# First layers of the compressions with 32 activation columns stationary on four column groups

## The chip, the core and the metric

The kernel runs on one core of one Trainium2 chip. The metric is the device time of one execution in microseconds; the times shown are the median of several executions, and a profile is one execution taken apart by the hardware profiler. The engines are named as the profile names them: PE is TensorE (PEld its weight loads), ACT ScalarE, DVE VectorE, POOL GpSimd, SP the engine that issues most transfers.

## The reference, cut to what matters

Two decoder layers on 512 positions of 1024 values. Each layer has an FFN, a mixer of three kinds of attention, a second FFN and an embedding gate. In the mixer, the NSA heads attend to compressed keys and values too. Each of 31 blocks (32 positions, a new one every 16) becomes one key and one value:

```
def compress(kv, pe, w1, w2):
    blk = kv[:, idx] + pe[:, None, :]
    blk = jnp.transpose(blk, (0, 1, 3, 2, 4)).reshape(B, n_cmp, NSA_KV_HEADS, CMP_BLOCK * HEAD_DIM)
    return jax.nn.gelu(blk @ w1) @ w2
kc = rope(compress(k_cmp, pos_k, phi_k1, phi_k2), block_end)
vc = compress(v_cmp, pos_v, phi_v1, phi_v2)
```

`blk @ w1` is the first layer: 31 rows (padded to 32) by 2048, times 2048 by 256. There are four of them in an execution: keys and values, in two layers. They are computed in full four-byte precision.

## The kernel before

Most products of the kernel split a four-byte operand into a high and a low part and add three products of a faster four-byte type. The first layers of the compressions don't: their operands are plain four-byte values, for which a matmul leaves two records in the trace, each with its own weight load.

The mixer (from L559) is written as a list of short steps, `SEQ`; the steps of one layer are written out in that order, and a scheduler then sets the order on each engine by priority and by when it holds inputs and buffers to be free. Each engine runs its own list strictly in that order. The steps that matter here:

- `cmp` (L800): projects the values to be compressed and lays them out as `xs`, sixteen slices of 128 by 32 for keys and for values.
- `hk0` to `hk3` and `hv0` to `hv3`: `phi(i, j)` (L819), a quarter of the first layer each. A step takes one weight unit of 128 by 1024 (`wraw`, loaded over SP into a buffer of its own) with four blocks of 256 columns. Before the change, each half block of 128 columns is stationary and 32 columns of `xs` move, eight matmuls per step, 32 per compression. All add up in one PSUM tile with tag "g", of which there are two; the projections and the compressed scores use the same two. Behind the last quarter VectorE takes the sums out as `gx` (L831) and a tanh GELU runs in nine small steps over VectorE and ScalarE (L834 to L846), which gives `g`.
- `ck` and `cv`: the second layers (`phik` with `gx`, `phiv` with `g`); `ck` gives `kp`, `cv` gives `vc`.
- `cs` and `ct`: the scores of the compressed keys (`nq`,`kp`), their softmax (`scr`, `sc`) and its transposition (`pct`). `pct`,`vc` is added to the output of an NSA head in the step `Pn0b`.
- `Q..`, `T..`, `P..`: scores and softmax, transposes and output product of a head. Names with n, d, f are NSA, differential and forgetting heads; `nk`,`nq` are the scores of NSA heads, `PT`,`VN` their output products, `ident`,`P` the transposes.
- `Gf..`, `Gd..`: the projection of a head, 24 matmuls of 512 columns (`xh`,`whi` and the like). `Gd0` is followed by a rotation: ScalarE copies to `raw_r` (L732), two transfers write `rot`, VectorE multiplies and adds (L735 to L737), ScalarE and VectorE split into `dhi` and `dlo`.

The steps between `hk2` and `Gf2` stand in `SEQ` as: hk2 hk3 Gf3 Qn1a hv0 hv1 ck Qn1b hv2 Tn0b Tn0a Pf1 Pn0a cs Gd0 hv3 ct Qn2a Qn2b Tn1b Qn3a cv Pn0b Tn1a Pn1a Qn3b Gf2.

Small working tiles come from a pool `tmp` of four buffers: `raw_r`, `rot`, `dhi`, `dlo`, `scr`, `sc` and others share them.

Of the kernel before, what the change touches and what calls it, by code (L numbers as in the profile page):

```python
# [20 lines left out]
F32 = mybir.dt.float32  # L21
F32R = mybir.dt.float32r
AF = mybir.ActivationFunctionType
# [29 lines left out]
def _mix(w, n):  # L53

    return w.reshape(-1, n, 2, 64 // n).transpose(0, 2, 3, 1).reshape(-1, 128)
# [61 lines left out]
def _consts():  # L117
    c = {}
    c["ident"] = np.eye(128, dtype=np.float32)
    q = np.arange(128)  # L120
    m = np.zeros((128, 512), np.float32)
    m[:, 384:] = np.where(q[None, :] <= q[:, None], 0.0, NEG)
    c["mask"] = m
    ut = np.ones((128, 512), np.float32)
    ut[:, :128] = (q[:, None] <= q[None, :])
    c["ut"] = ut

    def table(d, pos):
        inv = (np.float32(10000.0) ** (-np.arange(0, d, 2, dtype=np.float32) / np.float32(d))).astype(np.float32)
        ang = pos.astype(np.float32)[:, None] * inv[None, :]  # L130
        co, si = np.cos(ang).astype(np.float32), np.sin(ang).astype(np.float32)
        n = 128 // d
        return [np.ascontiguousarray(_mix(np.tile(np.concatenate(x, 1), (1, n)), n).T)
                for x in ((co, co), (-si, si))]

    t = np.arange(S)
    c["rope"] = np.stack([*table(64, t), *table(32, t)])
    be = np.arange(32) * 16 + 31
    c["ropec"] = np.stack(table(64, be), 1)
    ok = (np.arange(32)[None, :] < NCMP) & (be[None, :] <= t[:, None])  # L140
    c["maskc"] = np.where(ok, 0.0, NEG).astype(np.float32).reshape(4, 128, 32).transpose(1, 0, 2)
    c["rowc"] = (t >= 31).astype(np.float32).reshape(4, 128).T
    b = np.zeros((128, 128), np.float32)
    b[:64, :64] = b[64:, 64:] = 1.0 / 64
    c["bd"] = b
    return {k: np.ascontiguousarray(v, np.float32) for k, v in c.items()}


def layout(a):

    a = {k: np.asarray(v) for k, v in a.items()}
    o = dict(_consts())
    o["x"] = a["x"][0]
    o["xt"] = a["x"][0].T.reshape(KC, 128, S).transpose(1, 0, 2)
    o["pt"] = a["p"][:, 0].transpose(0, 2, 1).reshape(L, 2, 128, S).transpose(0, 2, 1, 3)
    o["ws"] = np.stack(_stream(a, 0) + _stream(a, 1))
    o["ln_g"], o["ln_b"], o["bg"] = a["ln_g"], a["ln_b"], a["ple_b_gate"]
    k2 = a["nsa_phi_k2"].reshape(L, 2, 128, 2, 32)
    o["phik2"] = np.stack([np.repeat(x.reshape(L, 2, 128, 64), 2, 3) for x in (k2, k2[..., ::-1, :])], 3).transpose(0, 2, 1, 3, 4)
    o["phiv2"] = a["nsa_phi_v2"].reshape(L, 2, 128, 64).transpose(0, 2, 1, 3)  # L160
    o["pe"] = np.stack([a["nsa_pos_k"], a["nsa_pos_v"]], 1).reshape(L, 2, 16, 128).transpose(0, 3, 1, 2)
    o["bf"] = a["fox_b_f"]
    o["lam"] = a["diff_lambda"].reshape(L, 128)
    o["sg"] = np.concatenate([a["diff_subln_g"]] * 2, 1)
    return {k: np.ascontiguousarray(v) for k, v in o.items()}
# [3 lines left out]
class _Body:  # L169
# [85 lines left out]
    def mm(self, out, l, r, start, stop, loose=False):  # L255

        self.nc.tensor.matmul(out, l, r, start=start, stop=stop, skip_group_check=loose)  # L257
# [361 lines left out]
    def mixer(self, l):  # L619
        nc, A = self.nc, self.A  # L620
# [18 lines left out]
        M = {}  # L639
# [21 lines left out]
        for t in range(NT):  # L661
            p = self.ps("gs"[t % 2])
# [155 lines left out]
        def phi(i, j):  # L818

            if j == 0:  # L820
                M["ps", i] = self.ps("g")
            p = M["ps", i][:, 0:64]
            w = self.unit().rearrange("p (b m n) -> p b m n", b=4, m=2)
            for b in range(4):
                k = 4 * j + b
                for m in range(2):
                    self.mm(p[:, 32 * m:32 * m + 32], w[:, b, m], M["X"][:, i, k], k + m == 0, k == 15, True)
            if j < 3:
                return
            x, y = lw([128, 2, 32], f"gx{i}"), lw([128, 2, 32], f"gy{i}")  # L830
            nc.vector.tensor_copy(x, p.rearrange("p (a b) -> p a b", a=2))  # L831

            c = 2.0 * math.sqrt(2.0 / math.pi)
            nc.vector.tensor_mul(y, x, x)  # L834
            nc.vector.tensor_scalar(y, y, -0.044715 * c, -c, op0=ALU.mult, op1=ALU.add)
            nc.vector.tensor_mul(y, y, x)
            nc.vector.tensor_scalar(y, y, 80.0, None, op0=ALU.min)
            nc.scalar.activation(y, y, AF.Exp)
            nc.vector.tensor_scalar(y, y, 1.0, None, op0=ALU.add)
            nc.vector.reciprocal(y, y)  # L840
            if i == 0:
                nc.vector.tensor_mul(x, x, y)
                M["phi", 0] = x
            else:
                g = M["phi", 1] = lw([128, 2, 4, 32], "g1")
                nc.vector.tensor_mul(g, *(a[:, :, None, :].to_broadcast([128, 2, 4, 32]) for a in (x, y)))  # L846
# [246 lines left out]
        for n in SEQ:  # L1093
            if n[0] == "W":
                out_piece(int(n[1]), int(n[2]))
            elif n[0] == "h":
                phi("kv".index(n[1]), int(n[2]))
            elif n in steps:
                steps[n]()
                if len(M) and all(k in M for k in (("q", 0), ("q", 1), "k")) and "n0" not in M:  # L1100
                    ready()
            else:
                {"G": G, "Q": QS, "T": TP, "P": PV}[n[0]](n[1:])
# [12 lines left out]
        g, b = self.bcast(A["ln_g"][l, 1]), self.bcast(A["ln_b"][l, 1])  # L1116
# [55 lines left out]
    def start(self):  # L1172
        nc, A = self.nc, self.A

        self.ident = self.cp.tile([128, 128], F32, name="ident")
        self.mhalf = self.cp.tile([128, 1], F32, name="mhalf")
        self.one = self.cp.tile([128, 1], F32, name="one")
        self.eps = self.cp.tile([128, 1], F32, name="eps")
        for n in ("mask", "bd", "maskc", "rowc", "ropec"):
            setattr(self, n, self.cp.tile(list(A[n].shape), F32, name=n))  # L1180
        self.xh = self.cp.tile([128, KC, S], F32R, name="xh")
        self.xl = self.cp.tile([128, KC, S], F32R, name="xl")
        nc.vector.memset(self.mhalf, -0.5)
        self.x = [self.h4(F32, name="x") for t in range(NT)]

        z = self.h4(shape=(128, 512), name="zero")
        nc.vector.memset(z.bitcast(F32), 0.0)
        p = self.ps("t")
        for _ in range(self.opt["warm"]):
            self.mm(p, z[:, 0:128], z, True, True)  # L1190

        raw = [self.h4(F32, name="raw") for _ in range(2)]
        for u in range(2):
            self.hl[u] = [self.big(self.tags[u], name="w") for _ in range(2)]
        for k in range(KC):
            r = self.big("h", F32, (128, 512), "xraw")
            x = nc.sync.dma_start(r, A["xt"][:, k])
            if k % 2 == 0:
                c = slice(128 * k, 128 * k + 256)
                for u in range(2):  # L1200
                    self.last_raw = nc.sync.dma_start(raw[u][:, c], A["ws"][u, :, c])
            self.hilo(self.xh[:, k], self.xl[:, k], r)
            if k % 2 == 0:
                for u in range(2):
                    self.hilo(self.hl[u][0][:, c], self.hl[u][1][:, c], raw[u][:, c])
        self.dma_u = self.split_u = 2
        for u in range(2, 4):
            self._load(u)
            self.after(self.last_raw, x)
            self.dma_u += 1  # L1210
        self.ahead(3)
        nc.vector.memset(self.one, 1.0)
        nc.vector.memset(self.eps, EPS)

    def load_x(self):
        nc, A = self.nc, self.A
        for t, n in ((self.ident, A["ident"]), *((self.x[t], A["x"][128 * t:128 * t + 128]) for t in range(NT)),
                     *((getattr(self, n), A[n]) for n in ("mask", "bd", "maskc", "rowc", "ropec"))):
            self.after(nc.sync.dma_start(t, n), self.last_raw)


# [72 lines left out]
```

## Time and profile before

| | us |
|---|---|
| median of 3 executions | 2094.37 (2089.83 to 2094.72) |
| profiled execution, time | 2092.3 |
| profiled execution, span | 2090.5 |
| PE busy | 2068.9 |
| PEld busy | 1840.6 |
| DVE busy | 1443.9 |
| ACT busy | 1107.8 |

The span runs from the first to the last instruction; the time of that execution holds 1.8 us more. The mixer of layer 0 lies at about 380 to 655 us, that of layer 1 at about 1420 to 1695 us. A timeline row gives the start, the duration (of a merged row, from its first start to its last end, with the pipeline's latency), engine, line, operation, output and inputs, shapes and count. On PE, "out<-a,b" has the moving operand first and the stationary second; "128*8" is the size of the stationary block. Because matmuls overlap in the pipeline, the distance of two starts is what a matmul costs, not its duration.

### The profile page before, as it was taken

Reading aid. Unit: us, or ns where it says so; the run is one execution under the profiler, and the core shown is the slowest. Engines: PE = TensorE matmul, PEld = TensorE weight load, DVE = VectorE, ACT = ScalarE, POOL = GpSimd, SP = SyncE. Lnnn points to the kernel's source line nnn. Section 1 sums busy time; section 2 is a strip of 40 time slices with the busy share of each in tenths; the row PEclk is TensorE's granted clock in tenths of the full one; section 3 lists DMA queues with packets and bytes.
Section 4 is the critical chain, followed back from the end, with each engine's and each line's share of the span. In section 5 each row is a group of like instructions: output and inputs, shape, how many; then the busy total and the mean of one; then the engine's idle time right before and its main releaser. Section 6 shows DMA issues by size and latency. Waiting matters only on the chain.

```text
span 2090.5 us, 32936 instructions
## 1 busy us (share of the span) xinstructions
PE 2068.9 (99%) x12727; PEld 1840.6 (88%) x12727; DVE 1443.9 (69%) x2674; ACT 1107.8 (53%) x1947; POOL 128.6 (6%) x165
## 2 busy tenths in 40 slices
PE   9999999999999999999999999999999999999999
PEld 7999888797778999988899998887977789998887
DVE  7797526359888888626768885364688879886275
ACT  5665424457874666513546654244678646664132
POOL 0000001000100000000000000010101000000000
PEclk9999999989999999999999999999999999999999
DMA  5765234544562655324226542355445526553241
GB/s 178 205 173 141 94 111 157 172 134 128 138 199 64 172 158 162 118 94 151 102 71 173 161 132 92 115 168 158 145 121 147 187 65 186 153 142 105 98 151 61
DMA packets 89821, 286.32 MB, mean 137 GB/s; under 512 B 12865, under 2 KB 15041, under 8 KB 89665
## 3 DMA queue, kind: packets, MB, share of 16 engines
q1 hardware_dynamic: 74864, 230.74, 32.2%
q0 software_dynamic: 14800, 53.48, 13.4%
q8 instruction: 100, 1.64, 0.3%
q14 instruction: 57, 0.46, 0.1%
HBM read 209.46 MB, written 6.29 MB: 103 GB/s over the span
## 4 chain that ended last, share of the span: by engine, by line
PE 89%; ACT 4%; DVE 3%; DMA 2%; issue 1%; SPq 0%; DVEq 0%; ACTq 0%; POOLq 0%
PE ps L257 86%; PE ps L951 2%; PE ps L274 1%; ACT whi L221 1%; ACT P L929 1%; DMA rot<-raw_r 1%; DMA raw<-in_ws_dram 1%; DVE wlo L227 1%; ACT PT L249 0%; DMA glo<-raw 0%; PE ps L998 0%; DMA xraw<-in_xt_dram 0%; DVE P L927 0%; DVE PT L250 0%; ACT ob L990 0%
## 5 line engine op out<-in xcount | busy, mean ns | idle before, releaser
L257 PE MATMUL ps<-whi,hl 128*128 128x512 f32 x1376 | 427.9, 390 | 0.0
L221 ACT ACTIVATE whi<-raw 128x1024 fp32r<-128x1024 f32 x198 | 209.3, 1059 | 389.6 <-PE ps L257 313.5
L227 DVE TENSOR_TENSOR wlo<-raw,whi 128x1024 fp32r<-128x1024 f32 x174 | 212.1, 1222 | 294.1 <-ACT whi L221 285.6
L257 PE MATMUL ps<-T,sum 128*128 128x256 f32 x2592 | 335.9, 283 | 0.0
L257 PEld LDWEIGHTS ps<-T,sum 128*128 128x128 f32 x2592 | 321.6, 192 | 1.1 <-ACT sum L388 0.7
L257 PEld LDWEIGHTS ps<-whi,hl 128*128 128x128 f32 x1376 | 257.7, 188 | 54.1 <-DVE hl L250 1.2
L257 PE MATMUL ps<-wlo,hl 128*128 128x512 f32 x704 | 274.1, 389 | 0.0
L391 DVE TENSOR_TENSOR sum<-whole,sum 128x512 fp32r<-128x512 f32 x288 | 194.3, 687 | 28.8 <-ACT sum L388 28.3
L388 ACT ACTIVATE sum<-whole 128x512 fp32r<-128x512 f32 x288 | 174.9, 627 | 49.0 <-DVE whole L426 28.4
L257 PE MATMUL ps<-xh,whi 128*128 128x512 f32 (+1 forms) x536 | 197.1, 370 | 0.8 <-ACT xh L276 0.8
L257 PE MATMUL ps<-xh,wlo 128*128 128x512 f32 (+1 forms) x536 | 195.9, 366 | 0.0
L257 PE MATMUL ps<-xl,whi 128*128 128x512 f32 (+1 forms) x536 | 195.7, 366 | 0.0
L257 PE MATMUL ps<-xh,glo 128*128 128x256 f32 x576 | 163.1, 283 | 0.2 <-DMA glo<-raw 0.2
L257 PE MATMUL ps<-xl,ghi 128*128 128x256 f32 x576 | 163.0, 283 | 0.0
L257 PE MATMUL ps<-xh,ghi 128*128 128x256 f32 x576 | 163.0, 283 | 0.0
L257 PEld LDWEIGHTS ps<-wlo,hl 128*128 128x128 f32 x704 | 132.2, 188 | 27.5
L929 ACT ACTIVATE P<-P,sst 128x128 f32<-128x128 f32 x192 | 106.5, 559 | 40.5 <-DVE sst L927 40.2
L398 ACT ACTIVATE ghi<-raw 128x1024 fp32r<-128x1024 f32 x72 | 76.2, 1058 | 76.7 <-PE ps L257 69.0
L257 PE MATMUL ps<-T,up 128*128 128x256 f32 x864 | 115.4, 283 | 0.0
L257 PE MATMUL ps<-xh,sum 128*128 128x256 f32 x576 | 115.4, 283 | 0.0
L257 PEld LDWEIGHTS ps<-xh,whi 128*128 128x128 f32 x536 | 101.2, 190 | 15.4 <-ACT xh L276 1.5
L927 DVE CUSTOM_DVE_ANT_0 P<-ps,mask 128x128 f32<-128x128 f32 x192 | 88.3, 485 | 38.2 <-PE ps L257 26.5
(245 smaller groups left out, 4033.4 us busy)
## 6 DMA issues: line engine op xcount, KB each, us to landing
raw<-in_ws_dram SPq DMA_DIRECT2D x270, 512.0 KB
P<-in_ws_dram SPq DMA_DIRECT2D x72, 512.0 KB
glo<-raw POOLq DMA_DIRECT2D x71, 512.0 KB, 4.7
wlo<-raw POOLq DMA_DIRECT2D x24, 512.0 KB, 5.1
wraw<-in_ws_dram SPq DMA_DIRECT2D x16, 512.0 KB
dx<-x SPq DMA_DIRECT2D x8, 512.0 KB
x<-dx SPq DMA_DIRECT2D x8, 512.0 KB
rot<-raw_r SPq DMA_DIRECT2D x28, 128.0 KB
```

Of the source, the lines that this page charges most:

```text
L221: self.nc.scalar.activation(hi, r, AF.Copy)
L227: self.nc.vector.tensor_sub(lo, r, hi.bitcast(F32))
L257: self.nc.tensor.matmul(out, l, r, start=start, stop=stop, skip_group_check=loose)
L274: nc.tensor.transpose(p[:, j], self.x[t][:, 128 * k:128 * k + 128], self.ident)
L388: S.activation(Sm[j, i][0], W[j, i], AF.Copy)
L391: V.tensor_sub(Sm[j, i][1], W.pop((j, i)), Sm[j, i][0].bitcast(F32))
L398: S.activation(h, g, AF.Copy)
L927: nc.vector.tensor_tensor_reduce(v, p[:, 0:n], self.mask[:, 512 - n:512], -scale, 3e38, ALU.add, ALU.min, nm[:, t:t + 1])
L929: nc.scalar.activation(v, v, AF.Exp, bias=nm[:, t:t + 1], scale=-1.0, accum_out=sm[:, t:t + 1])
L951: nc.tensor.transpose(p[:, 128 * i:128 * i + 128], P[:, off[t] + 128 * kb:off[t] + 128 * kb + 128], self.ident)
```

## The change

`phi` swaps the operands of the first layer. The 32 columns of `xs` are stationary and a whole block of 256 weight columns moves: four matmuls per step instead of eight. The four blocks of a step write four different groups of 32 PSUM partitions, hence four column groups of the array. Each group adds up its own four of the sixteen slices over the four steps. After the last step ScalarE copies the 128 by 256 sums to a tile `qs` from the pool `tmp`, and two matmuls with `qs` stationary and four stacked identities `four` (128 by 32) moving add the four parts, into another part of the same PSUM tile. The rest is as before. `four` is one more constant, loaded with the others in the first FFN.

```
--- before.py
+++ after.py
@@ -143,6 +143,7 @@
     b = np.zeros((128, 128), np.float32)
     b[:64, :64] = b[64:, 64:] = 1.0 / 64
     c["bd"] = b
+    c["four"] = np.tile(np.eye(32, dtype=np.float32), (4, 1))
     return {k: np.ascontiguousarray(v, np.float32) for k, v in c.items()}
 
 
@@ -819,14 +820,19 @@
 
             if j == 0:
                 M["ps", i] = self.ps("g")
-            p = M["ps", i][:, 0:64]
-            w = self.unit().rearrange("p (b m n) -> p b m n", b=4, m=2)
+            q = M["ps", i][:, 0:256]
+            w = self.unit().rearrange("p (b n) -> p b n", b=4)
+
             for b in range(4):
-                k = 4 * j + b
-                for m in range(2):
-                    self.mm(p[:, 32 * m:32 * m + 32], w[:, b, m], M["X"][:, i, k], k + m == 0, k == 15, True)
+                self.mm(q[32 * b:32 * b + 32], M["X"][:, i, 4 * j + b], w[:, b], j == 0, j == 3, True)
             if j < 3:
                 return
+
+            qs = self.tmp(shape=(128, 256), name="qs")
+            nc.scalar.activation(qs, q, AF.Copy)
+            p = M["ps", i][:, 256:320]
+            for m in range(2):
+                self.mm(p[:, 32 * m:32 * m + 32], qs[:, 128 * m:128 * m + 128], self.four, m == 0, m == 1, True)
             x, y = lw([128, 2, 32], f"gx{i}"), lw([128, 2, 32], f"gy{i}")
             nc.vector.tensor_copy(x, p.rearrange("p (a b) -> p a b", a=2))
 
@@ -1180,6 +1186,7 @@
             setattr(self, n, self.cp.tile(list(A[n].shape), F32, name=n))
         self.xh = self.cp.tile([128, KC, S], F32R, name="xh")
         self.xl = self.cp.tile([128, KC, S], F32R, name="xl")
+        self.four = self.cp.tile([128, 128], F32, name="four")[:, 0:32]
         nc.vector.memset(self.mhalf, -0.5)
         self.x = [self.h4(F32, name="x") for t in range(NT)]
 
@@ -1215,7 +1222,7 @@
     def load_x(self):
         nc, A = self.nc, self.A
         for t, n in ((self.ident, A["ident"]), *((self.x[t], A["x"][128 * t:128 * t + 128]) for t in range(NT)),
-                     *((getattr(self, n), A[n]) for n in ("mask", "bd", "maskc", "rowc", "ropec"))):
+                     *((getattr(self, n), A[n]) for n in ("mask", "bd", "maskc", "rowc", "ropec", "four"))):
             self.after(nc.sync.dma_start(t, n), self.last_raw)
```

The scheduler's order changes from the first compression to the end of each mixer. On PE, layer 0, from `hk1` to the end of `hk3` (`xs`,`wraw` is the old product, `wraw`,`xs` the new one), the kernel before has:

```order
L257 MATMUL ps<-xs,wraw 128x32 x8
L257 MATMUL ps<-nk,nq 128x128
L257 MATMUL ps<-nk,nq 128x256
L257 MATMUL ps<-xs,wraw 128x32 x13
L257 MATMUL ps<-nkl,nq 128x128
L257 MATMUL ps<-nkl,nq 128x256
L257 MATMUL ps<-xs,wraw 128x32 x3
```

In the changed kernel the same stretch of PE's list reads:

```order
L258 MATMUL ps<-wraw,xs 32x256 x4
L258 MATMUL ps<-nk,nq 128x128
L258 MATMUL ps<-nk,nq 128x256
L258 MATMUL ps<-wraw,xs 32x256 x5
L258 MATMUL ps<-nkl,nq 128x128
L258 MATMUL ps<-nkl,nq 128x256
L258 MATMUL ps<-wraw,xs 32x256 x3
```

The counts halve and the shape changes; the score products stand between them at nearly the same places.

On ACT, layer 0, about the rotation of `Gd0` (`raw_r`, `dhi`) and the GELU of the value compression (`gy`, then `vc` from the second layer), the kernel before has:

```order
L249 ACTIVATE oT<-pair 128x512
L895 ACTIVATE sc<-sc 128x512
L732 ACTIVATE raw_r<-ps 128x512
L838 ACTIVATE gy_4845<-gy_4845 128x64
L221 ACTIVATE whi<-raw 128x1024
L224 ACTIVATE wlo<-raw 128x1024
L249 ACTIVATE vc<-ps 128x64
L249 ACTIVATE PT<-ps 128x512 x2
L249 ACTIVATE PT<-ps 128x256
L249 ACTIVATE dhi<-raw_r 128x512
```

In the changed kernel, from the exponentials ahead of `dhi`:

```order
L935 ACTIVATE P,sst<-P,sst 128x384
L250 ACTIVATE PT<-ps 128x512
L935 ACTIVATE P,sst<-P,sst 128x512
L250 ACTIVATE dhi<-raw_r 128x512
L250 ACTIVATE PT<-ps 128x256
L832 ACTIVATE qs<-ps 128x256
L844 ACTIVATE gy_4823<-gy_4823 128x64
L935 ACTIVATE P,sst<-P,sst 128x128
L935 ACTIVATE P,sst<-P,sst 128x256
L250 ACTIVATE pct<-ps 128x512
L935 ACTIVATE P,sst<-P,sst 128x384
L250 ACTIVATE vc<-ps 128x64
```

Before, `gy` and `vc` of the value compression stand ahead of `dhi`; now the copy `qs`, `gy` and `vc` stand behind it.

On PE, layer 0, about the second layer of the value compression (`phiv`). In the kernel before, the end of an output product stands ahead of it and Gf2's projection behind it:

```order
L257 MATMUL ps<-PT,VN 128x128
L257 MATMUL ps<-PT,VN 64x128
L257 MATMUL ps<-phiv,g_4854 128x64 x2
L257 MATMUL ps<-xh,whi 128x512
L257 MATMUL ps<-xl,whi 128x512
L257 MATMUL ps<-xh,wlo 128x512
L907 MATMUL ps<-ident,sc 128x128 x4
L951 MATMUL ps<-ident,P 128x128 x8
```

In the changed kernel `phiv` stands among these:

```order
L258 MATMUL ps<-nkl,nq 128x256
L957 MATMUL ps<-ident,P 128x128 x2
L258 MATMUL ps<-four,qs 128x32 x2
L957 MATMUL ps<-ident,P 128x128 x4
L258 MATMUL ps<-nk,nq 128x384
L258 MATMUL ps<-nkl,nq 128x384
L258 MATMUL ps<-nk,nq 128x512
L258 MATMUL ps<-nkl,nq 128x512
L957 MATMUL ps<-ident,P 128x128 x4
L258 MATMUL ps<-nk,nq 128x128
L258 MATMUL ps<-nkl,nq 128x128
L258 MATMUL ps<-phiv,g_4832 128x64 x2
L258 MATMUL ps<-xh,whi 128x512
```

Before, `Gd0`'s projection ends 13 rows ahead of `phiv` (at row 1643 of the list, `phiv` is row 1656), and transposes and Gf2's projection follow it. Now `Gd0`'s projection ends 33 rows ahead (1647 and 1680): transposes, scores, output products and the identities stand between, and Gf2's projection begins behind `phiv`.

## Rows read from the trace of the kernel before

**Rows 1.** The page, busy time by engine and the chain that ended last.

```profile
PE 2068.9 (99%) x12727; PEld 1840.6 (88%) x12727; DVE 1443.9 (69%) x2674; ACT 1107.8 (53%) x1947; POOL 128.6 (6%) x165
...
PE 89%; ACT 4%; DVE 3%; DMA 2%; issue 1%; SPq 0%; DVEq 0%; ACTq 0%; POOLq 0%
```

**Rows 2.** Groups by form on PE: count, busy us, mean ns, idle before.

```profile
L257 PE MATMUL ps<-xs,wraw 128*128 128x32 f32 x256 | 34.0, 292 | 0.0
```

**Rows 3.** Timeline of PE, 420 to 480 us.

```profile
424.54 1.87 PE L257 MATMUL ps<-xs,wraw 128*128 128x32 f32 x16
426.24 0.31 PE L257 MATMUL ps<-fb,fa 128*128 128x128 f32 x1
```

**Rows 4.** PE by stretch: length, busy us (count), mean granted clock, DMA share, GB/s.

```profile
436.00:448.00 12.00, 12.00 (x67) 0.72 0.59 208
456.00:464.00 8.00, 8.00 (x40) 0.57 0.44 91
478.90:494.40 15.50, 13.94 (x81) 1.00 0.73 188
494.40:616.20 121.80, 117.90 (x640) 1.00 0.49 145
1480.00:1486.00 6.00, 6.00 (x29) 0.72 0.73 251
1494.00:1502.00 8.00, 8.00 (x41) 0.57 0.47 97
1618.00:1620.00 2.00, 0.77 (x2) 1.00 0.77 272
1620.00:1624.00 4.00, 3.98 (x14) 0.57 1.00 212
```

**Rows 5.** Timeline of PE at the decay sum.

```profile
392.50 2.32 PE L257 MATMUL ps<-ut,fz 128*8 128x512 f32 x8
394.75 0.50 PE L257 MATMUL ps<-xh,whi 128*128 128x512 f32 x1
```

**Rows 6.** Timeline of the weight loads (PEld) at the decay sum.

```profile
392.94 0.09 PEld L257 LDWEIGHTS ps<-ut,fz 128*8 128x8 f32 x1 [0.34 <-issue]
393.37 0.09 PEld L257 LDWEIGHTS ps<-ut,fz 128*8 128x8 f32 x1 [0.34 <-issue]
```

**Rows 7.** Timeline of PE, 478 to 496 us.

```profile
478.44 0.39 PE L257 MATMUL ps<-xl,whi 128*128 128x512 f32 x1
478.67 0.39 PE L257 MATMUL ps<-xh,wlo 128*128 128x512 f32 x1
...
479.36 1.32 PE L257 MATMUL ps<-PT,VN 128*128 128x512 f32 x8
481.17 0.66 PE L257 MATMUL ps<-phiv,g 128*128 128x64 f32 x4 [0.49 <-DVE g L846]
...
487.56 0.34 PE L257 MATMUL ps<-nk,nq 128*128 128x384 f32 x1
...
488.37 0.39 PE L257 MATMUL ps<-xl,whi 128*128 128x512 f32 x1
...
494.37 0.50 PE L257 MATMUL ps<-pct,vc 32*128 32x512 f32 x1
```

**Rows 8.** Timeline of ACT, 478 to 490 us.

```profile
481.53 1.06 ACT L221 ACTIVATE whi<-raw 128x1024 fp32r<-128x1024 f32 x1 [1.69 <-DMA raw<-in_ws_dram]
...
487.06 0.38 ACT L249 ACTIVATE PT<-ps 128x256 fp32r<-128x256 f32 x1 [2.44 <-PE ps L951]
487.34 0.62 ACT L249 ACTIVATE dhi<-raw_r 128x512 fp32r<-128x512 f32 x1
```

**Rows 9.** Timeline of DVE, 467 to 482 us: the value compression's GELU.

```profile
467.72 0.23 DVE L831 COPY gx<-ps 128x64 f32<-128x64 f32 x1 [0.87 <-PE ps L257]
...
475.65 0.22 DVE L834 TENSOR_TENSOR gy<-gx 128x64 f32<-128x64 f32 x1
...
480.69 0.42 DVE L846 TENSOR_TENSOR g<-gx,gy 128x256 f32<-128x256 f32 x1
```

More of the change, by code (lines that the diff above doesn't have):

```diff
@@ L145, in _consts @@
     c["bd"] = b
+    c["four"] = np.tile(np.eye(32, dtype=np.float32), (4, 1))
     return {k: np.ascontiguousarray(v, np.float32) for k, v in c.items()}
@@ L821, in phi @@
                 M["ps", i] = self.ps("g")
-            p = M["ps", i][:, 0:64]
-            w = self.unit().rearrange("p (b m n) -> p b m n", b=4, m=2)
+            q = M["ps", i][:, 0:256]
+            w = self.unit().rearrange("p (b n) -> p b n", b=4)
             for b in range(4):
-                k = 4 * j + b
-                for m in range(2):
-                    self.mm(p[:, 32 * m:32 * m + 32], w[:, b, m], M["X"][:, i, k], k + m == 0, k == 15, True)
+                self.mm(q[32 * b:32 * b + 32], M["X"][:, i, 4 * j + b], w[:, b], j == 0, j == 3, True)
             if j < 3:
                 return
+            qs = self.tmp(shape=(128, 256), name="qs")
+            nc.scalar.activation(qs, q, AF.Copy)
+            p = M["ps", i][:, 256:320]
+            for m in range(2):
+                self.mm(p[:, 32 * m:32 * m + 32], qs[:, 128 * m:128 * m + 128], self.four, m == 0, m == 1, True)
             x, y = lw([128, 2, 32], f"gx{i}"), lw([128, 2, 32], f"gy{i}")
@@ L1182, in start @@
         self.xl = self.cp.tile([128, KC, S], F32R, name="xl")
+        self.four = self.cp.tile([128, 128], F32, name="four")[:, 0:32]
         nc.vector.memset(self.mhalf, -0.5)
@@ L1217, in load_x @@
         for t, n in ((self.ident, A["ident"]), *((self.x[t], A["x"][128 * t:128 * t + 128]) for t in range(NT)),
-                     *((getattr(self, n), A[n]) for n in ("mask", "bd", "maskc", "rowc", "ropec"))):
+                     *((getattr(self, n), A[n]) for n in ("mask", "bd", "maskc", "rowc", "ropec", "four"))):
             self.after(nc.sync.dma_start(t, n), self.last_raw)
```

## The prediction

> **What bounds the kernel now.** I read the page first: TensorE is busy 99% of the span and carries 89% of the chain that ended last [rows 1]. So TensorE time is span, unless another engine or a buffer is late. The groups by form price what the change replaces: the 128 matmuls of the compressions' first layers leave 256 records (two per four-byte matmul), 34.0 us busy [rows 2]. The timeline gives their pitch: 16 records fill 424.54 to 426.24, 0.106 us each, though each moves 32 columns only [rows 3]. At that pitch one layer's 128 records cost 13.6 us. The third view, busy time and granted clock by stretch, shows more. Where these records stand nearly alone the granted clock falls to the lower of its two levels (1.2 of 2.4 GHz), and the matmuls behind them pay too. Layer 0: 12 us at mean clock 0.72 and 8 us at 0.57; layer 1: 6 us at 0.72 and 8 us at 0.57 [rows 4]. Time times (1 - clock): 3.4 + 3.4 = 6.8 us and 1.7 + 3.4 = 5.1 us. TensorE is busy throughout these stretches, so this is its own time. At stake: 13.6 + 6.8 = 20.4 us in layer 0, 13.6 + 5.1 = 18.7 us in layer 1, 39.1 us or 1.9% of the span.
>
> **The new first layer.** 64 matmuls (128 records) with 32 stationary and 256 moving columns. No row shows this shape, nor two matmuls on different column groups beside each other. The nearest is the decay sum: eight stationary columns, four-byte data, records of 512 columns 0.43 us apart (392.94 to 393.37) [rows 6]. Half the columns, half the time: a record of 256 is 0.215 us, and a matmul two. Upper bound, nothing overlaps: 0.43 us per matmul, 13.8 us per layer, just what the old records cost at full clock. Lower bound, all four groups overlap: 0.108 us, 3.4 us. I take the middle, 0.215 us, 6.9 us per layer, because of the order of the records: the two of one matmul share a column group and stand one behind the other, so the second has to wait for the first. If records start in queue order, the next matmul's first record can start only beside that second one, and only two streams ever run. This is reasoned, not shown.
>
> Going into the narrow shape and out again costs something. The decay's eight records (two each of 512, 384, 256 and 128 columns: 2.15 us by the price above) last until 394.75, 2.25 us, and the full-width record behind them takes 0.50 us, where its kind takes 0.39 us [rows 5, 7]. I take 0.2 us per episode, between 0.1 and 0.3; the order of the changed kernel has seven episodes per layer: 1.4 us. The rows alone don't say whether the narrow block or something else at that place costs this. The Trainium skill (TensorEngine Tiling (Array Packing), Key Properties) says that a change of tiling mode drains the engine, which speaks against this change: by it every episode pays. Without it both layers would be 2.8 us cheaper.
>
> The added identities: two matmuls per compression, eight records per layer in the old shape, at 0.106 us: 0.85 us. New TensorE time per layer: 6.9 + 1.4 + 0.85 = 9.1 us. I expect the full clock here, since 256-column streams leave no gaps. Saved ahead of the waits: 20.4 - 9.1 = 11.3 us and 18.7 - 9.1 = 9.6 us, **20.9 us together**.
>
> Small parts. ScalarE gets four copies of 128x256, 0.38 us each [rows 8]. The key compression's stands behind an exponential of Qn1a, with eight projection matmuls (0.23 us each, 478.44 to 478.67 [rows 7]) on TensorE between that head's last scores and the identities; that covers it, else it costs up to 0.5 us. The added load of `four` is one issue on SP's queue in the first FFN, far from its use: nothing, or the one issue. In the new order ScalarE's copies of `kp` stand behind a `wlo`, and `scr` behind a `whi`; such a copy of 128x1024 takes 1.06 us [rows 8], and a TensorE that arrives early waits for them: 2 us per layer, between 0 and 3. Left: 16.9 us.
>
> **What comes later instead.** The value compression decides. Before, its `gx` is taken out of PSUM at 467.72, its `g` is done at 481.1, TensorE waits 0.49 us for it at 481.17, and `pct`,`vc` starts at 494.37, while Gf2's projection fills the gaps [rows 7, 9]. After, the copy `qs` needs one of the four `tmp` buffers. On ScalarE it stands behind `dhi` of Gd0, thus behind Gd0's whole rotation, and on TensorE nothing of Gf2's projection stands ahead of `phiv`. The length of that way, from rows: Gd0's last matmul starts at 478.67 and ScalarE ends `dhi` at 487.96, 9.3 us [rows 7, 8]; `PT` and `qs`, 0.8 us; the identities, as long as the four records of `phiv`, 0.7 us [rows 7]; the GELU, 5.5 us (475.65 to 481.1, queued among softmax work as it will be again [rows 9]). `phiv` comes 16.3 us behind Gd0's last matmul, where it came 2.5 us behind.
>
> What TensorE has for those 16.3 us, by the order: eight `PT`,`VN` (1.3 us, 479.36 to the wait), 32 transposes at 0.106 us (3.4 us), two groups of long scores (0.81 us each, 487.56 to 488.37) and three short pairs (0.6 us), the identities (0.4 us): 7.3 us [rows 7]. It idles 9.0 us. In the same place it idled 15.50 - 13.94 = 1.56 us before [rows 4]. New idling: about 7 us per layer, **14 us**. The bounds are 7 us (half) and 18 us (nothing of it hidden).
>
> Two corrections. A gap can pull the clock down: behind 1618 to 1620, where TensorE was busy 0.77 of 2.00 us, four microseconds ran at 0.57, a loss of 1.7 us [rows 4]. One such fall per layer: 3.4 us, between 0 and 7. In return TensorE idles 121.80 - 117.90 = 3.9 us per layer in the rest of the mixer, waiting for softmax [rows 4]; VectorE and ScalarE get about 7 us ahead of it now, so I give back half, 4 us, between 0 and 7.8.
>
> **Sum.** -20.9 + 4 (small waits) + 14 + 3.4 - 4 = **-3.5 us**. The profiled execution took 2092.3 us with a span of 2090.5 us; the median is 2094.37 us, 0.1% above it. I put the difference on the median: 2091 us, -0.2%. About 0.3% (6.3 us) is what a measurement of this kernel can tell from no change, so the forecast is no change that can be told.
>
> **Rivals.**
> (a) All four groups overlap. For it: nothing in the code ties the groups together, each writes its own 32 partitions. Against it: the pairs of records. It is worth 0.108 us per matmul, 3.4 us per layer: -10.3 us, 2084 us. The Trainium skill (TensorE: Matmul & The Clock Gate, Part 3) is on this side: matmuls on different column groups start some 4 ns apart, and three of them gained 2.38 times. No run here shows it yet.
> (b) The new idling stays at its lower end, 7 us, since the rotation's steps find emptier queues, and no clock falls. Then 14 + 3.4 - 4 becomes 7 + 0 - 4: -13.9 us, 2080 us. For it: VectorE and ScalarE wait on TensorE at several places ahead of Gd0. Against it: the rotation's transfer and vector work are not TensorE's to shorten.
> (c) The change doesn't do what it says: the groups run one behind the other. Its place is the 64 matmuls, its price 0.215 us more for each, 13.8 us: +10.3 us, 2105 us, slower. The clock's gain alone doesn't pay for the idling. It ends slower than 0.3% from a price of 0.37 us per matmul on: 9.8 us above the forecast, over 64. For it: no row shows overlap.
>
> **How the numbers follow.** Forecast 0.40, (a) 0.22, (b) 0.18, (c) 0.20. Around each I allow 5 us for the idling and for the changed order of the rest of the mixer. Faster than 2088 us: 0.10 of the forecast's 0.40, 0.16 of (a), 0.12 of (b): 0.38. Slower than 2101 us: 0.03 of the forecast's and 0.13 of (c): 0.16. Within: 0.46. The range leaves out the far halves of (b) and (c), 0.19 together: 2080 to 2105 us. The forecast's own range is 2085 to 2097 us.
>
> **What would show it.** The new records: starts of one column group's next matmul 0.215 us on (forecast), 0.108 (a) or 0.43 (c), and a granted clock of 1.00 where it was 0.72 and 0.57. The wait: a gap of several microseconds on TensorE ahead of `four`,`qs` and of `phiv`, released by ScalarE's `qs` and VectorE's `g`; `phiv` some 16 us behind Gd0's last matmul. If that gap is under 3 us, or the later idling grows instead of falling, the step on the value compression is wrong.

## The result: slower by 0.7%, and the profile after

| | before | changed |
|---|---|---|
| median, us | 2092.48 (4 runs, 2089.83 to 2094.72) | 2107.94 (4 runs, 2104.07 to 2113.17) |
| ratio, 95% interval | 1 | 1.0069 [1.0052, 1.0086] |
| profiled execution, span | 2090.5 | 2102.3 |

The forecast was 2091 us and its range ended at 2105. The page of the changed kernel, first line busy time, second the chain that ended last, answers to [rows 1]:

```profile
PE 2060.3 (98%) x12615; PEld 1813.1 (86%) x12615; DVE 1445.4 (69%) x2674; ACT 1107.9 (53%) x1951; POOL 127.3 (6%) x165
...
PE 88%; ACT 4%; DVE 3%; DMA 3%; issue 2%; SPq 0%; DVEq 0%; ACTq 0%; POOLq 0%
```

TensorE is busy 8.6 us less and the span is 11.8 us longer: it idles 20.4 us more. Where, the trace of layer 0 tells in three steps. First the new products, on TensorE's timeline (start, duration, engine, line, operation, out<-moving,stationary, shapes, count, and in brackets the idle time before):

```profile
423.00 0.64 PE L258 MATMUL ps<-wraw,xs 128*32 128x256 f32 x8
423.57 0.33 PE L258 MATMUL ps<-fb,fa 128*128 128x128 f32 x1
...
433.85 1.05 PE L258 MATMUL ps<-wraw,xs 128*32 128x256 f32 x10
434.83 0.50 PE L258 MATMUL ps<-nkl,nq 128*128 128x128 f32 x2
...
444.99 1.50 PE L258 MATMUL ps<-wraw,xs 128*32 128x256 f32 x24
446.42 1.31 PE L957 MATMUL ps<-ident,P 128*128 128x128 f32 x10
...
450.28 0.62 PE L258 MATMUL ps<-wraw,xs 128*32 128x256 f32 x2
450.83 1.08 PE L258 MATMUL ps<-gx,phik 128*128 128x32 f32 x8
```

Read the distance from each first start to the next row's start: 8 records (four matmuls, four groups) take 0.57 us, 24 take 1.43, but 2 take 0.55 and 10 take 0.98. That is 0.43 us for each round of up to four matmuls, and 0.12 to 0.14 us for going in and out. So all four groups overlap, and an incomplete round costs as much as a full one. The seven episodes take 5.2 us, near the 4.8 us that rival (a) asked for (3.4 us and 1.4 us of episodes), and the granted clock is 1.00 throughout (first row below), where [rows 4] had 0.72 and 0.57. Gd0's last projection matmul starts at 466.49; before, at 478.67 [rows 7]. By then the changed kernel is 12.2 us ahead. Not all of that is the change: 1.6 us were there before the first compression (the decay sum starts at 390.88, and before at 392.50 [rows 5]).

Second, what lies behind it. TensorE by stretch: length, busy us (count), granted clock, DMA share, GB/s:

```profile
423.00:467.00 44.00, 42.49 (x264) 1.00 0.65 190
466.90:487.20 20.30, 13.93 (x70) 0.75 0.48 135
487.20:621.30 134.10, 125.14 (x649) 0.99 0.42 123
...
476.60:480.60 4.00, 2.52 (x8) 0.50 0.51 180
480.60:484.90 4.30, 3.89 (x12) 0.50 0.28 101
```

The second row answers to 478.9:494.4 of [rows 4], the third to 494.4:616.2. TensorE idles 6.4 us from Gd0's end to `pct`,`vc` (before 1.6) and 9.0 us in the rest (before 3.9). Behind a gap of 4.1 us the clock stands at its lower level, 1.2 GHz, for 8.3 us. The gap on the timelines of TensorE, VectorE, ScalarE and SP's queue:

```profile
466.49 0.39 PE L258 MATMUL ps<-xh,wlo 128*128 128x512 f32 x1
...
472.17 0.30 PE L957 MATMUL ps<-ident,P 128*128 128x128 f32 x1
476.58 0.58 PE L258 MATMUL ps<-nk,nq 128*128 128x256 f32 x1 [4.11 <-DVE sst L933]
479.22 1.06 PE L258 MATMUL ps<-four,qs 128*128 128x32 f32 x4 [0.75 <-ACT qs L832]
485.17 0.61 PE L258 MATMUL ps<-phiv,g 128*128 128x64 f32 x4
487.17 0.73 PE L258 MATMUL ps<-pct,vc 32*128 32x512 f32 x2
...
474.62 0.69 DVE L736 TENSOR_TENSOR raw_r<-raw_r,rope 128x512 f32<-128x512 f32 x1 [2.78 <-DMA rot<-raw_r]
475.83 0.69 DVE L933 CUSTOM_DVE_ANT_0 P<-ps,mask 128x512 f32<-128x512 f32 x1
...
477.28 0.61 ACT L250 ACTIVATE dhi<-raw_r 128x512 fp32r<-128x512 f32 x1
478.79 0.38 ACT L832 ACTIVATE qs<-ps 128x256 f32<-128x256 f32 x1
...
469.68 1.12 SPq L735 DMA_DIRECT2D rot<-raw_r  x2
```

VectorE stands still 2.78 us for the rotation's transfer. Behind it, in its list, is the masking of the scores (`P<-ps,mask`) that must give TensorE a bank back. TensorE has nothing else: Gf2's projection is queued behind `phiv`, `phiv` behind the GELU, the GELU behind the identities, and these behind `qs`, which stands behind `dhi`. `phiv` starts 18.7 us behind Gd0's last matmul. Third: `pct`,`vc` still starts 7.2 us earlier than before (487.17 against 494.37), but 22 fewer projection matmuls are done by then, 5 us of work that comes later; and the rest of the layer idles more, as the third stretch shows. The next FFN's first stretch starts 5.8 us later (655.23 and 661.02); by the end of layer 1's mixer the difference is 11.7 us (1695.57 and 1707.22).

### The profile page after: what moved, and what is told of

Read it like the earlier page. It is cut to its first block, busy times and chain, and to the rows that moved or that the text cites. A ratio compares the mean times of both kernels' runs of the same rounds, so it can differ in the third digit from the quotient of the medians.

```text
span 2102.3 us, 32722 instructions
## 1 busy us (share of the span) xinstructions
PE 2060.3 (98%) x12615; PEld 1813.1 (86%) x12615; DVE 1445.4 (69%) x2674; ACT 1107.9 (53%) x1951; POOL 127.3 (6%) x165
## 4 chain that ended last, share of the span: by engine, by line
PE 88%; ACT 4%; DVE 3%; DMA 3%; issue 2%; SPq 0%; DVEq 0%; ACTq 0%; POOLq 0%
PE ps L258 86%; PE ps L957 1%; DMA raw<-in_ws_dram 1%; PE ps L275 1%; ACT whi L222 1%; DVE wlo L228 1%; ACT P L935 1%; DMA rot<-raw_r 1%; ACT PT L250 1%; DMA glo<-raw 0%; DVE P L933 0%; ACT ob L996 0%; PE ps L1004 0%; DMA wlo<-raw 0%; DMA xraw<-in_xt_dram 0%
## 5 line engine op out<-in xcount | busy, mean ns | idle before, releaser
L258 PEld LDWEIGHTS ps<-xh,wlo 128*128 128x128 f32 x536 | 101.3, 189 | 15.5 <-issue 1.3
```

## The experiments

All times are against the kernel before on the same chip. Two questions lead through them: do the products or the way of adding the parts move the time, and by which wait? Theory 1 says that the detour of the sums through the shared buffer loses the time, theory 2 that VectorE and ScalarE set the pace, so that TensorE time saved turns into waiting.

**Products and adding apart.** Two runs make a square of old and new products with and without the detour of the sums through a shared buffer. `noadd` has the new products without copy and identities, so it leaves out the adding of the four parts:

```
-            qs = self.tmp(shape=(128, 256), name="qs")
-            nc.scalar.activation(qs, q, AF.Copy)
-            p = M["ps", i][:, 256:320]
-            for m in range(2):
-                self.mm(p[:, 32 * m:32 * m + 32], ...)
+            p = M["ps", i][:, 0:64]
```

> New products in the old order: the changed kernel without the copy and the identities; the GELU's input is taken straight from the first 64 columns of the unadded sums, so the adding of the four parts is left out. TensorE's list between the products is that of the kernel before at the value compression (phiv ahead of the rotation's end). Theory 1: what the products save is kept: about 28.6 us by 0.06 us per new record, 0.106 per old one and the clock, minus some 3 us of small waits: 2064 to 2074 us. Theory 2: the saved TensorE time turns into waits for softmax: 2085 to 2096 us.

`oldwait` is the kernel before with the detour:

```
-            nc.vector.tensor_copy(x, p.rearrange("p (a b) -> p a b", a=2))
+            qs = self.tmp(shape=(128, 256), name="qs")
+            nc.scalar.activation(qs[:, 0:64], p, AF.Copy)
+            nc.vector.tensor_copy(x, qs[:, 0:64].rearrange("p (a b) -> p a b", a=2))
```

> Old products in the new order: the kernel before, with its sums taken through a tile of the pool tmp (a copy on ScalarE) before the GELU; the list of TensorE behind Gd0 is then nearly that of the changed kernel. Theory 1: the wait costs without the new products what it costs with them, some 40 us: 2122 to 2138 us. Theory 2: the old products leave no time to lose, so the detour costs its copies alone: 2092 to 2098 us.

| ratio to before | no detour | detour |
|---|---|---|
| old products | 1 | 1.0163 [1.0149, 1.0178], 2127.14 us |
| new products | 0.9894 [0.9881, 0.9907], 2071.77 us | 1.0069 [1.0052, 1.0086] |

Both times lie where theory 1 put them. The products give 1.06% without the detour and 0.94% with it, 22 and 20 us. The detour costs 1.63% with the old products and 1.75% with the new, 34 and 37 us; with the new ones it holds the identities too, 3.4 us of TensorE by form. So saved TensorE time isn't turned into waiting (theory 2 falls); the detour loses more than the products win. In `noadd` the timeline behind Gd0 repeats [rows 7] 11.4 us earlier:

```profile
469.75 0.66 PE L258 MATMUL ps<-phiv,g 128*128 128x64 f32 x4 [0.49 <-DVE g L848]
```

In `oldwait` the gap of the changed kernel stands there with the old products:

```profile
487.76 0.39 PE L257 MATMUL ps<-nk,nq 128*128 128x256 f32 x1 [3.60 <-DVE sst L929]
490.75 0.69 PE L257 MATMUL ps<-nk,nq 128*128 128x384 f32 x1 [1.10 <-DVE sst L929]
```

**One column group.** `onegroup` is `own_d` (below) with the same 64 matmuls all in one group; copy and identities take the 32 partitions that are left (not shown):

```
-                self.mm(q[32 * b:32 * b + 32], M["X"][:, i, 4 * j + b], w[:, b], j == 0, j == 3, True)
+                self.mm(q[0:32], M["X"][:, i, 4 * j + b], w[:, b], j + b == 0, j + b == 6, True)
```

> As own_d, but all sixteen slices of a compression are added up in one column group (32 partitions) instead of four, and the two identities add nothing but a copy: the same 64 matmuls of the same shape, no two of them on different groups. If the four groups overlap, as the 0.06 us per record in the changed kernel say, a record comes every 0.215 us here (half of the decay sum's 0.43) and the first layers cost 64 x (0.43 - 0.12) = 20 us more. If the groups had nothing to do with the pitch, it stays at 0.06 us.

2099.85 us in one run, 18 us above `own_d`. On TensorE, four matmuls and then three:

```profile
435.04 1.91 PE L258 MATMUL ps<-wraw,xs 128*32 128x256 f32 x8
436.89 0.33 PE L258 MATMUL ps<-nk,nq 128*128 128x128 f32 x1
...
439.10 1.48 PE L258 MATMUL ps<-wraw,xs 128*32 128x256 f32 x6
440.52 0.33 PE L258 MATMUL ps<-nk,nq 128*128 128x128 f32 x1
```

1.85 us and 1.42 us: one matmul is 0.43 us, the upper bound of the prediction, and 0.13 us go for the episode. By form the 128 records are 31.4 us busy here and 11.4 us in the changed kernel: 20 us for the overlap, as expected. The scheduler ordered other work differently in this run, so the time bears only roughly on it; the pitch does.

**The buffer, and where hv3 stands.** `own` gives `qs` a buffer of its own, `own_seq` also moves hv3 ahead of Gd0 in `SEQ` (`cs hv3 Gd0 ct`):

```
-            qs = self.tmp(shape=(128, 256), name="qs")
+            qs = lw([128, 256], "qs")
```

> The changed kernel with the copied sums qs in a buffer of their own instead of one of the four of the pool tmp, so that the value compression's copy stands ahead of raw_r on ScalarE and no longer behind dhi. Theory 1 (the time is lost by the value compression's copy, which waits for Gd0's rotation to give back a buffer; everything behind it follows): TensorE's waits ahead of the identities and of phiv fall under 1 us, the softmax waits behind them (DVE sst, 1.8 to 4.1 us each) under 1 us, and the time comes to 2070 to 2082 us. Theory 2 (VectorE's and ScalarE's softmax work sets the pace, so TensorE time saved in the mixer turns into waiting, with or without that copy): the waits only move, and the time stays within 6 us of the changed kernel's, 2102 to 2114 us.

> The same, and the last quarter of the value compression's first layer (hv3) stands ahead of Gd0 in the list of steps, so that the identities and phiv stand ahead of and right behind Gd0's projection. Theory 1: as own or 2 to 6 us better, since the tanh GELU then runs beside the 24 projection matmuls: 2066 to 2080 us. Theory 2: within 6 us of the changed kernel, 2102 to 2114 us.

`own`: 2090.23 us, 0.9984 [0.9975, 0.9993]; `own_seq`: 2078.53 us, 0.9926 [0.9914, 0.9938]. The second is as theory 1 expects; it computes everything and beats both kernels. The first lies between the theories. The buffer alone takes away half of the detour's cost. In `own` the copy runs early (ScalarE at 465.95), but the identities stay behind Gd0's 24 matmuls in TensorE's list, and VectorE stands still for the rotation's transfer as in the changed kernel:

```profile
470.63 0.53 PE L258 MATMUL ps<-four,qs 128*128 128x32 f32 x4
480.04 0.33 PE L258 MATMUL ps<-nk,nq 128*128 128x128 f32 x1 [1.93 <-DVE sst L933]
...
478.22 0.69 DVE L736 TENSOR_TENSOR raw_r<-raw_r,rope 128x512 f32<-128x512 f32 x1 [2.63 <-DMA rot<-raw_r]
```

In `own_seq` `phiv` starts 0.2 us behind Gd0's last matmul. What is left against `noadd` is 6.5 us at the end of layer 0 (651.80 and 645.27) and 6.9 us at the end of layer 1, so it arises in layer 0: a wait of 3.61 us for `sst` is the largest part, then the identities, twice some 0.5 us, and the waits at `kp`, 0.9 us.

**The engine that copies.** `tmp_d` is the changed kernel with `nc.vector.tensor_copy(qs, q)`, `own_d` the same with the buffer of its own.

> The changed kernel with the copy on VectorE, but still into a tile of the pool tmp. Theory A (the shared buffer is needed for the harm): the identities still stand far behind Gd0's projection, a wait of 3 us or more for DVE sst stays, 2100 to 2116 us. Theory B (the place of the copy in ScalarE's queue did the harm, not the buffer): 2072 to 2082 us.

> The changed kernel with qs in a buffer of its own and the copy on VectorE instead of ScalarE; the list of steps is the changed kernel's. On TensorE Gd0's projection is then split about the output product again (3, then 20), since the value compression's sums leave their bank of PSUM before the compressed scores leave theirs. Theory A (what costs is how long the sums keep their bank of PSUM: the projections behind them can't fill the rotation's time): the wait for DVE sst behind Gd0 falls from 4.1 us (changed kernel) and 1.9 us (own buffer, ScalarE) to under 1 us, the time to 2072 to 2080 us. Theory B (an engine more or less busy makes no difference once the buffer is free): as with the copy on ScalarE, 2087 to 2093 us.

`tmp_d` 2097.46 us, 1.0018 [1.0008, 1.0027]; `own_d` 2081.44 us, 0.9940 [0.9926, 0.9954]. With either engine the shared buffer costs: 2097 against 2081 on VectorE, 2108 against 2090 on ScalarE. The engine is worth about 10 us beside it, which neither theory had. Theory A's times are missed by 2.5 us in `tmp_d` (with a wait for `sst` of 2.42 us, not 3) and by 1.4 us in `own_d`, and there its reason by more: a wait of 4.76 us for `sst` is left (4.40 in layer 1), though the bank is free early.

**hv3 earlier still.** `s2d` and `s1d` are `own_d` with hv3 right behind hv2, or ahead of `cs`.

> As own_d (own buffer, copy on VectorE), with hv3 moved from behind Gd0 to right behind hv2 in the list of steps. The identities stand ahead of the compressed scores and phiv between the parts of Gd0's projection. Theory A: with the bank free even earlier nothing is left to gain but the small waits at kp (0.6 and 0.3 us), so 2070 to 2080 us, within 4 us of own_d. Theory B: 2087 to 2093 us. Against both: the weights of hv3 are asked for earlier and those of Gd0 later on SP's queue; if they come late, TensorE waits for DMA there, 1 to 4 us per layer.

> As the kernel with qs in its own buffer and copied by VectorE, with hv3 ahead of the compressed scores in the list of steps. TensorE's list behind Gd0 is then that of the run without the adding, but for a few rows: phiv stands two output products later and Gf2's matmuls stand among the score products. If the order of those rows is what the 10 us between the two runs hang on: 2073 to 2078 us, with no wait over 1.5 us behind Gd0. If it is the adding itself (copy, identities): 2080 to 2084 us.

2082.73 us, 0.9944 [0.9932, 0.9957], and 2080.35 us, 0.9945 [0.9931, 0.9958]: the same as `own_d`. Theory A's time for `s2d` is missed by 2.7 us; `s1d` has the time expected if the adding itself costs. The 4.8 us wait is gone in both, and others stand in its place in layer 0:

```profile
460.97 0.50 PE L258 MATMUL ps<-PT,VN 128*128 128x512 f32 x1 [2.54 <-ACT PT L250]
571.19 0.85 PE L258 MATMUL ps<-dk,dq 96*128 96x384 f32 x2 [2.75 <-DVE sst L933]
```

for `s2d`, and for `s1d`

```profile
472.12 0.50 PE L258 MATMUL ps<-xh,whi 128*128 128x512 f32 x1 [2.14 <-ACT raw_r L733]
573.85 0.84 PE L258 MATMUL ps<-dk,dq 96*128 96x384 f32 x2 [2.74 <-DVE sst L933]
```

In these two runs no single wait is the cost: where the order takes one away, others come out.

**Freeing VectorE.** The three operations of Gd0's rotation go to GpSimd in the changed kernel (`rp_after`), in the kernel before (`rp_before`) and in `own_d` (`rp_d`):

```
-            r = rope(project(), M["t32"])
+            r = rope(project(), M["t32"], nc.gpsimd if h == 0 else nc.vector)
```

> The changed kernel with the two multiplications and the addition of Gd0's rotation on GpSimd instead of VectorE, nothing else. Theory V (the 4.1 us wait for DVE sst behind Gd0 is VectorE standing still in its own list for the rotation's transfer, with the next head's masking of scores queued behind): that wait falls under 1 us and the time by 4 to 10 us, to 2098 to 2104 us. Theory P (TensorE lacks work there, since the value compression keeps its bank of PSUM until its copy has a buffer and Gf2's projection can't start): the idle time only moves to other waits between Gd0's last matmul and phiv, which stays over 15 us behind it; 2104 to 2112 us.

> The kernel before with Gd0's rotation on GpSimd in the same way: what this move is worth where TensorE has Gf2's projection beside the rotation. Both theories: VectorE's standing still is covered there, only the 1.1 us wait for DVE PT per layer can go: 2090 to 2095 us.

> The kernel with qs in its own buffer and copied by VectorE (2081 us), and Gd0's rotation on GpSimd. There a wait of 4.8 us (layer 0) and 4.4 us (layer 1) for DVE sst is left behind Gd0. Theory V: both fall under 1 us, 2070 to 2076 us. Theory P: they are replaced by other waits, 2079 to 2084 us.

2113.97 us, 1.0108 [1.0090, 1.0126]; 2112.63 us, 1.0091 [1.0075, 1.0108]; 2096.63 us, 1.0016 [1.0007, 1.0025]: all slower than without the move, by 6, 19 and 15 us. No time is one that V or P expects. In `rp_after` the wait only moves, as P has it:

```profile
475.25 0.44 PE L258 MATMUL ps<-nk,nq 128*128 128x384 f32 x1 [0.39 <-DVE sst L933]
480.77 1.06 PE L258 MATMUL ps<-four,qs 128*128 128x32 f32 x4 [4.38 <-ACT qs L832]
484.49 0.58 PE L258 MATMUL ps<-nk,nq 128*128 128x256 f32 x1 [2.17 <-DVE sst L933]
...
475.57 1.27 POOL L736 TENSOR_TENSOR raw_r<-raw_r,rope 128x512 f32<-128x512 f32 x1 [2.79 <-DMA rot<-raw_r]
480.10 0.69 DVE L251 TENSOR_TENSOR dlo<-raw_r,dhi 128x512 fp32r<-128x512 f32 x1 [4.50 <-ACT dhi L250]
```

GpSimd takes 1.27 us for what VectorE does in 0.69 us, and VectorE waits for `dlo` instead. In `rp_d` a wait of 7.56 us for VectorE's `PT` stands where one of 4.76 us for `sst` stood. The move thus lengthens the rotation that it was to take off VectorE, so V's gain doesn't come, but V isn't refuted. `rp_before` loses 19 us; its TensorE idles 34.3 us, where it idled 21.6 us before, and is busy 9.6 us more. From which step that comes is open.

**Bank or path.** `hold` is `noadd` with an unused copy of the value sums to a shared tile, so that only their bank of PSUM is kept; `path` (the second diff, against the changed kernel) frees the bank at once and keeps the long way; `tb_s1` has neither: it is `path` without the second copy, and with hv3 ahead of `cs`.

```
+            if i == 1:
+                nc.scalar.activation(self.tmp(shape=(128, 256), name="qs"), q, AF.Copy)
```

```
+            qs = lw([128, 256], "qq")
+            nc.vector.tensor_copy(qs, q)
+            if i == 1:
+                qq, qs = qs, self.tmp(shape=(128, 256), name="qs")
+                nc.scalar.activation(qs, qq, AF.Copy)
+            p = self.ps("t")[:, 0:64]
```

> New products; the GELU takes its input straight from the first 64 columns of the unadded sums (the adding is left out), but behind it the value compression's sums are still copied by ScalarE to an unused tile of the pool tmp. So the bank of PSUM is kept until Gd0's rotation is done, as in the changed kernel, while the GELU and phiv are as early as without the adding (2072 us). Theory H (the bank kept is what costs): most of the 36 us between that run and the changed kernel, 2095 to 2108 us. Theory L (what costs is that the path from the sums to phiv runs through the copy behind the rotation, and with it Gf2's projection, which is queued behind phiv): 2072 to 2080 us.

> The other half: VectorE copies the sums to a buffer of their own at once, so that their bank is free early, and ScalarE copies them on from there, for the values, to a tile of the pool tmp, behind dhi of Gd0's rotation as in the changed kernel; the identities write another bank. Gd0's projection can start between the compressed scores again, but the identities, the GELU and phiv still wait for the rotation. Theory H: 2074 to 2086 us. Theory L: phiv stays 12 us or more behind Gd0's last matmul with waits of 4 us or more in between, 2095 to 2108 us.

> Neither: VectorE copies the sums to a buffer of their own, the identities write another bank of PSUM, and hv3 stands ahead of the compressed scores in the list of steps. By both theories nothing of the harm is left: 2073 to 2080 us, above the run without the adding (2072 us) by the identities (0.85 us per layer by the price of the prediction) and the four copies, 0.42 us each on VectorE, where they are waited for. If the time stays at 2081 us or more, the rest hangs on neither bank nor path.

`hold` 2084.71 us, 0.9957 [0.9941, 0.9974]; `path` 2129.68 us, 1.0162 [1.0139, 1.0185]; `tb_s1` 2100.42 us, 1.0036 [1.0023, 1.0048]. The bank, with the copy that keeps it, costs 13 us of the 36: less than H, more than L. `path` goes the way of L and far beyond it, and `tb_s1` meets neither. The traces say why the sizes can't be read as bank and path. In `path`, TensorE, then ScalarE, then VectorE, then SP's queue (start, and how long the two issues took with their wait):

```profile
484.25 1.06 PE L258 MATMUL ps<-four,qs 128*128 128x32 f32 x4 [14.54 <-ACT qs L835]
...
482.40 0.63 ACT L250 ACTIVATE dhi<-raw_r 128x512 fp32r<-128x512 f32 x1 [10.42 <-DVE raw_r L738]
...
480.29 0.69 DVE L736 TENSOR_TENSOR raw_r<-raw_r,rope 128x512 f32<-128x512 f32 x1 [9.75 <-DMA rot<-raw_r]
...
465.63 7.18 SPq L209 DMA_DIRECT2D raw<-in_ws_dram  x2
472.90 1.13 SPq L735 DMA_DIRECT2D rot<-raw_r  x2
```

The rotation's transfers stand on SP behind two weight loads that hold the queue until 472.8, though `raw_r` was written at 468.9: 4.0 us late, where the changed kernel's (469.68) were 1.2 us late. From there to VectorE's start 7.4 us pass; in the changed kernel, 4.9 us. In `tb_s1` TensorE waits for an order on ScalarE:

```profile
471.15 1.06 ACT L222 ACTIVATE whi<-raw 128x1024 fp32r<-128x1024 f32 x1 [6.75 <-DMA raw<-in_ws_dram]
472.11 0.24 ACT L844 ACTIVATE gy<-gy 128x64 f32<-128x64 f32 x1
```

The GELU's exponential (`gy`) stands behind a weight split that waits for its transfer, and TensorE waits 5.16 us for `g` at 474.09. Before, `gy` stood ahead of that split, and the split waited 1.69 us [rows 8]. The weights come 10.4 us earlier than before (471.15 and 481.53), Gd0's last matmul 11.7 us (466.93 and 478.67). `s1d` differs from `tb_s1` only in the bank that the identities write; there `gy` runs ahead of the split, and the time is 20 us shorter. So one small edit can move the time by more than the bank, through the order that the scheduler makes; that all 20 us come from this place is not shown.

What stays open: how the 36 us divide between the bank, the longer way to `phiv` and the order that the scheduler makes of the rest. That the detour through the shared buffer costs them, and that an own buffer with hv3 ahead of Gd0 returns 30 of them, is shown.

## Why the prediction was wrong

For both layers, in us, forecast against the two profiled executions (layer 1 in the same two stretches, 1515.7 to 1534.7 and 1534.7 to 1666.0 against 1516.9 to 1532.4 and 1532.4 to 1655.0):

| term | forecast | measured |
|---|---|---|
| old products and their clock | -39.1 | gone, clock 1.00 |
| new products with episodes | +16.6 | +11.4 |
| identities | +1.7 | +3.4 |
| small waits | +4 | +3.0 |
| idling at the value compression | +14 | +8.5 |
| clock, there and later | +3.4 | +9.0 |
| idling later | -4 | +7.6 |
| sum | -3.5 | about +4 of +11.8 |

New products and identities are the busy time of their groups by form. Idle is length less busy time; the small waits are the idle time up to Gd0's end, 1.5 us in each layer. The clock costs half of the busy time at its lower level. In the changed kernel these are four stretches (TensorE, columns as above):

```profile
474.69:484.94 10.25, 6.48 (x21) 0.50 0.39 128
583.92:587.34 3.42, 3.32 (x9) 0.50 1.03 260
1526.00:1532.83 6.83, 5.72 (x20) 0.50 0.38 145
1628.40:1635.23 6.83, 5.89 (x16) 0.50 0.89 220
```

That is 10.7 us, less the 1.7 us that [rows 4] have behind 1620. Some 8 us of the difference are in none of the terms. By the terms (old and new products, identities, clock) TensorE's busy time falls by 15.3 us, by the two pages by 8.6 us: the other matmuls, the same in number (12727 - 256 and 12615 - 144), are busy some 7 us longer. Why is not shown.

- **Price of the products: wrong, to our cost nothing.** The pairing of records was the reason given for two streams, and it doesn't hold. Rival (a)'s mechanism is what happens; its time isn't, for the rest went against it. By the Trainium skill (TensorE: Matmul & The Clock Gate, Part 3) matmuls on different column groups run together; the trace agrees: 12 matmuls in 1.43 us, of 0.43 us each. Rival (c) falls; that its 2105 us is the rival's time nearest to the measured one is luck.
- **Episodes: over-sized.** 0.12 to 0.14 us instead of 0.2. The Trainium skill (TensorEngine Tiling (Array Packing), Key Properties) has a change of tiling mode drain the engine. By this trace it costs at most these 0.14 us. A round begun and broken off for other matmuls costs more, up to 0.43 us.
- **The wait on the rotation: right in place, mechanism and distance.** `phiv` 18.7 us behind Gd0's last matmul (forecast 16.3), `qs` behind `dhi`, small waits at `kp` (3.0 us for 4). The new idling was over-sized, 8.5 against 14 us, near rival (b)'s 7; but (b) also has no clock fall, and there is one. The square of four runs shows that this detour loses the time, not the products.
- **The step that failed is what came after it.** The prediction gave back half of the later idling, since VectorE and ScalarE would be ahead. The idling grew, as the falsifier named. It measures +7.6 us where -4 was forecast. The clock's fall, taken from a place with a gap of 1.2 us [rows 4], was under-sized, 3.4 against 9.0 us: the gap is 4.1 us in one piece in layer 0, and 8.3 us ran at half clock behind it. Together these two are 17.2 us to the bad, against 10.7 us to the good from the products and the shorter idling.
- **The size of the detour was judged by its first wait.** It was costed at some 13 us (14 + 3.4 - 4) and measures 34 to 37 us. With `phiv` late the bank, Gf2's projection and the order of the steps behind move too; the runs show that each can cost (`hold` 13 us for the bank), not how the sum divides.

## What to carry to other kernels

Swapping a narrow moving operand into the stationary place and spreading it over four column groups pays here (22 us by `noadd`, 20 us with the detour in both kernels), and best if its matmuls come in whole rounds of four. But a result that has to pass a copy before it goes on needs a buffer that nothing late returns: an own buffer and an earlier place in the list turned +0.7% into -0.7%. When an added wait puts a projection behind it, cost what is queued behind, the clock after the gap, and the idling of the rest of the stage with a sign that may be either.

## What was not expected of the hardware

- A round of up to four matmuls on four column groups takes 0.43 us whether one or four are in it (2 records 0.55 us, 8 records 0.57 us, with the episode).
- A gap can cost clock on top of itself, and its length alone doesn't tell how much. Behind 4.1 us of idling TensorE ran 8.3 us at 0.50, 6.4 us of them busy; behind 3.6 us in `own_seq`, 4.6 us at 0.69; behind the gap of 1.93 us in `own` it stayed at 1.00; but behind 2.52 us in layer 1 of the changed kernel (TensorE starts again at 1523.98) the lower level came too, for 6.8 us (the third of the four stretches above). TensorE by stretch, `own_seq` and then `own`:

```profile
475.70:479.40 3.70, 0.09 (x2) 1.00 0.47 107
479.40:484.00 4.60, 4.58 (x17) 0.69 0.28 105
```

```profile
478.00:480.00 2.00, 0.11 (x1) 1.00 0.52 102
480.00:484.00 4.00, 3.93 (x21) 1.00 0.49 180
```
